# RMS norm with repeated rows: GpSimd in place of SyncE as the issuer of the loads of x and the stores

## The chip, the cores and the metric

The kernel runs on one core of a Trainium2 chip. The metric is device time in microseconds (us) of one execution. Before the change it was 238.1 us, the median of 3 runs (238.0 to 238.66). The engines are named as in the profile: DVE is VectorE, ACT is ScalarE, POOL is GpSimd, SP is SyncE; TensorE does no work in this kernel. An issue row of an engine's sequencer carries a q (SPq, POOLq).

## What is computed

```python
x: (8, 512, 2048) float32, gamma: (2048,) float32

def reference(x, gamma):
    x_rep = np.repeat(x, 2, axis=1)
    rms = np.sqrt((x_rep ** 2).mean(axis=-1, keepdims=True) + 1e-6)
    return ((x_rep / rms) * gamma[None, None, :]).astype(np.float32)
```

Each of 4,096 rows of 2,048 values is divided by its root mean square, multiplied by gamma, and written twice, to neighbouring rows of the output. 33.5 MB are read and 67.1 MB written.

## The kernel before

The rows lie in four blocks of 1,024 rows, numbered n = 0 to 3. A block is one load: each of the 128 partitions gets 8 neighbouring rows, 64 KB, in one transfer of 8.4 MB (`load`, L49 and L50). The output of a block is two stores, each of the doubled form of 4 rows per partition, again 64 KB per partition and 8.4 MB (`store`, L52 and L53). There are 4 loads and 8 stores, 12 transfers of one size.

All of it lives in one tile y of 24 rows of 2,048 values per partition, in three parts of 8 rows, `first` (rows 0 to 7), `second` (8 to 15) and `third` (16 to 23). `load(n, first + K)` fills rows 4 to 11, which is half of `first` and half of `second`; `load(m, third)` fills the third part. `squares` (L63, L67) sums the squares of a row on ACT and takes the root; `scale` (L76, L77) takes the reciprocal on DVE and multiplies the row by it and by gamma, writing the result to every second row of the target part; `repeat` (L84) copies these rows to the rows between, on ACT or on DVE.

The order is written by hand (`manual_schedule`), so that each engine takes its instructions as the code lists them. `four(n, m, constants, at_once)` handles two blocks: load n, the constants, load m, then rows 0 to 3 of n and store (n, 0), rows 4 to 7 and store (n, 1), and so for m. It is called with (0, 1) and then with (3, 2); the second call has no constants. In this text store (n, first half) is `store(n, 0, ...)`. The loads of the second call go to parts of y from which stores of the first call still read, and wait for those.

`constants()` brings gamma to one partition with four small DMAs on ACT's queue (one of 16 pieces of 500 bytes, L123, and three of 64 bytes, L129), into rows of y that are free at that time. POOL then spreads gamma to all partitions with two `partition_broadcast` instructions into gamma_b: L133 for the first 2,000 columns, which waits for the large piece, and L137 for the last 48, which waits for the small ones. In the code these stand between `load(n, ...)` and `load(m, ...)` of the first call. They are POOL's only work apart from four tiny fills and two configuration entries at the start.

Of the kernel before, what the change touches and what calls it, by code (L numbers as in the profile page):

```python
# [1 line left out]

# [4 lines left out]


@with_exitstack
def kernel(  # L10
    ctx: ExitStack,
    tc: tile.TileContext,
    x: bass.AP,
    gamma: bass.AP,
    out: bass.AP,
):
    nc = tc.nc
    P = nc.NUM_PARTITIONS
    f32 = mybir.dt.float32
    Act = mybir.ActivationFunctionType  # L20
    Alu = mybir.AluOpType

    B, S, D = x.shape
    Bo, So, Do = out.shape
    R = So // S
    assert R == 2 and D == Do and B == Bo and So == S * R
    eps = 1e-6
    inv_d = 1.0 / float(D)


    K = 4
    N = B * S
    ntiles = N // (P * K)
    assert N % (P * K) == 0 and ntiles == 8
    H = 2
    x_t = x.rearrange("b s d -> (b s) d").rearrange("(n p k) d -> n p k d", p=P, k=H * K)
    out_t = out.rearrange("b s d -> (b s) d").rearrange("(n p h j) d -> n h p (j d)", p=P, h=H, j=K * R)

    singles = ctx.enter_context(tc.tile_pool(name="singles", bufs=1))
    rows = ctx.enter_context(tc.tile_pool(name="rows", bufs=1))  # L40
    junk = ctx.enter_context(tc.tile_pool(name="junk", bufs=1, space=bass.MemoryType.PSUM))
    small = ctx.enter_context(tc.tile_pool(name="small", bufs=4))

    y = rows.tile([P, 3 * K * R, D], f32, name="y")
    first, second, third = 0, K * R, 2 * K * R

    def load(n, at):  # L49
        nc.sync.dma_start(out=y[:, at : at + H * K, :], in_=x_t[n])  # L50

    def store(n, h, to):  # L52
        nc.sync.dma_start(  # L53
            out=out_t[n, h], in_=y[:, to : to + K * R, :].rearrange("p j d -> p (j d)")
        )

    def squares(at, rows):

        n = len(rows)
        ss = small.tile([P, n], f32, name=f"ss{n}")  # L60
        for c, k in enumerate(rows):
            sq = junk.tile([P, D], f32, name="sq")
            nc.scalar.activation(  # L63
                out=sq[:], in_=y[:, at + k, :], func=Act.Square, accum_out=ss[:, c : c + 1]
            )
        rms = small.tile([P, n], f32, name=f"rms{n}")
        nc.scalar.activation(out=rms[:], in_=ss[:], func=Act.Sqrt, scale=inv_d, bias=eps_t[:])  # L67
        return rms

    def scale(at, to, rows, rms, at_once=K):  # L70
        n = len(rows)
        rstd = small.tile([P, n], f32, name=f"rstd{n}")
        for c, k in enumerate(rows):
            if c % at_once == 0:
                part = slice(c, min(c + at_once, n))
                nc.vector.reciprocal(out=rstd[:, part], in_=rms[:, part])  # L76
            nc.vector.scalar_tensor_tensor(  # L77
                out=y[:, to + R * k, :], in0=y[:, at + k, :], scalar=rstd[:, c : c + 1],
                in1=gamma_b[:], op0=Alu.mult, op1=Alu.mult,
            )  # L80

    def repeat(to, k0, k1, copy):
        y_r = y[:, to + R * k0 : to + R * k1, :].rearrange("p (k r) d -> p k r d", r=R)
        copy(out=y_r[:, :, 1, :], in_=y_r[:, :, 0, :])  # L84

    ctx.enter_context(tc.manual_schedule())

    half = K // 2
    up, down = list(range(K)), list(range(K - 1, -1, -1))

    def four(n, m, constants, at_once):


        load(n, first + K)
        constants()
        load(m, third)
        for rows, n_at_once in ((up[:half], half), (up[half:], at_once)):
            scale(first + K, first, rows, squares(first + K, rows), n_at_once)
        repeat(first, 0, half, nc.scalar.copy)
        repeat(first, half, K, nc.vector.tensor_copy)  # L100
        store(n, 0, first)
        scale(second, second, down, squares(second, down))
        repeat(second, half, K, nc.scalar.copy)
        repeat(second, 0, half, nc.vector.tensor_copy)
        store(n, 1, second)
        roots = [squares(third + h * K, up) for h in range(H)]
        scale(third, first, up, roots[0])
        repeat(first, 0, half, nc.scalar.copy)
        repeat(first, half, K, nc.scalar.copy)
        store(m, 0, first)  # L110
        scale(third + K, third, up, roots[1])
        repeat(third, 0, K, nc.scalar.copy)
        store(m, 1, third)

    gamma_b = singles.tile([P, D], f32, name="gamma_b")
    G, E = 16, 3
    C = D // G - E
    gamma_s = y[0:1, 0:2, :].rearrange("p k (c d) -> p (k c) d", c=G // 2)
    gamma_t = y[0:1, 2, :]
    eps_t = singles.tile([P, 1], f32, name="eps_t")  # L120

    def constants():
        nc.scalar.dma_start(  # L123
            out=gamma_s[0:1, :, :C],
            in_=gamma[: G * C].rearrange("(p c d) -> p c d", p=1, c=G),
        )
        for c in range(E):
            at = G * C + c * G
            nc.scalar.dma_start(  # L129
                out=gamma_t[0:1, c * G : (c + 1) * G],  # L130
                in_=gamma[at : at + G].partition_broadcast(1),
            )
        nc.gpsimd.partition_broadcast(  # L133
            out_ap=gamma_b[:, : G * C].rearrange("p (c d) -> p c d", c=G),
            in_ap=gamma_s[0:1, :, :C],
        )
        nc.gpsimd.partition_broadcast(out_ap=gamma_b[:, G * C :], in_ap=gamma_t[0:1, : E * G])  # L137
        nc.vector.memset(eps_t, eps)  # L138

        root = singles.tile([P, 1], f32, name="root")[:]  # L140
        nc.scalar.activation(out=root, in_=eps_t[:], func=Act.Sqrt)  # L141

    four(0, 1, constants, 1)
    four(3, 2, lambda: None, half)


# [1 line left out]
_INS = ['x', 'gamma']  # L148
_OUTS = [((8, 1024, 2048), 'float32')]


# [23 lines left out]
```

## Time and profile before

| | us |
|---|---|
| median of 3 runs | 238.1 |
| span of the profiled execution, first to last instruction | 236.3 |
| DVE busy | 84.5 |
| ACT busy | 110.2 |
| POOL busy | 2.8 |
| q1 (SP's queue: x and out) | 1,728 packets, 100.66 MB, 98.7% of 16 engines' span |
| q10 (ACT's queue: gamma) | 38 packets, 0.01 MB, 0.0% |
| loads of x, median from issue to landing | 31.4 |
| stores, median from issue to landing | 24.9 |
| HBM read and written | 33.56 MB, 67.11 MB: 426 GB/s over the span |

The span leaves out what lies before the first instruction and after the last one. The DMA share is the mean over the core's 16 DMA engines. A landing is the moment at which the transfer's semaphore is full; a transfer that stands behind others of its queue waits its turn within that time. Beside the page, the trace holds a record of each DMA packet (queue, size, start and duration).

### The profile page before, as it was taken

To read this page: it belongs to the slowest core of one execution; us is meant where nothing else is said; L and a number is where in the kernel's file an instruction comes from. 1 tells how busy PE (TensorE), PEld (TensorE's weight loads), DVE (VectorE), ACT (ScalarE), POOL (GpSimd) and SP (SyncE) were. 2 spreads that over 40 slices of the span, in tenths; PEclk is the share of its full clock that TensorE was granted. 3 is DMA by queue.
4 is the path that set the end of the run, shared out by engine and by line. 5 is a ranking of instruction groups with operands and counts; after the bars stand their busy time and mean duration, and the time that the engine had idled before them with its cause. 6 is when DMAs were issued, how large, how long until landed. Compare 5 with 4: busy or idle time off the path is not lost.

```text
span 236.3 us, 226 instructions
## 1 busy us (share of the span) xinstructions
DVE 84.5 (36%) x48; ACT 110.2 (47%) x86; POOL 2.8 (1%) x6
## 2 busy tenths in 40 slices
DVE  0000496594699500000000007928919992000000
ACT  2001989479998470000000049991999957400000
POOL 0110000000000000000000000000000000000000
DMA  9898989989898989989898998989898988989894
GB/s 355 356 533 355 521 366 477 411 366 521 355 533 356 499 388 466 422 366 521 355 533 355 488 399 355 533 355 533 355 533 355 499 388 377 510 355 533 355 533 178
DMA packets 1767, 100.68 MB, mean 426 GB/s; under 512 B 230, under 2 KB 230, under 8 KB 230
## 3 DMA queue, kind: packets, MB, share of 16 engines
q1 hardware_dynamic: 1728, 100.66, 98.7%
q10 hardware_dynamic: 38, 0.01, 0.0%
q14 instruction: 1, 0.01, 0.0%
HBM read 33.56 MB, written 67.11 MB: 426 GB/s over the span
## 4 chain that ended last, share of the span: by engine, by line
DMA 45%; ACT 26%; DVE 12%; issue 2%; DVEq 0%
DMA y<-in_x_dram 26%; DMA out_dram<-y 20%; ACT sq L63 15%; DVE y L77 12%; ACT y L84 11%; ACT rms L67 1%; DVE rstd L76 0%; DVEq L77 0%
## 5 line engine op out<-in xcount | busy, mean ns | idle before, releaser
L63 ACT ACTIVATE sq<-y 128x2048 f32<-128x2048 f32 x32 | 60.1, 1878 | 71.1 <-DMA y<-in_x_dram 70.4
L77 DVE SCALAR_TENSOR_TENSOR y<-y,rstd,gamma_b 128x2048 f32<-128x2048 f32 x32 | 73.8, 2349 | 1.6 <-DMA out_dram<-y 1.0
L84 ACT COPY y<-y 128x4096 f32<-128x4096 f32 (+1 forms) x10 | 42.6, 4284 | 19.1 <-DVE y L77 18.3
L76 DVE RECIPROCAL rstd<-rms 128x4 f32<-128x4 f32 (+2 forms) x11 | 1.9, 169 | 109.2 <-ACT rms L67 109.2
L84 DVE COPY y<-y 128x4096 f32<-128x4096 f32 x4 | 9.2, 2294 | 0.1
L63 ACT ACTIVATION_READ_ACCUMULATOR sq<-y 128x1 f32 x32 | 6.0, 186 | 0.0
L67 ACT ACTIVATE rms<-ss,eps_t 128x4 f32<-128x4 f32 (+1 forms) x10 | 3.0, 297 | 0.3
L141 ACT ACT_TABLE_LOAD x1 | 1.3, 1283 | 2.6 <-issue 2.6
L133 POOL PARTITION_BROADCAST gamma_b<-y x1 | 2.2, 2243 | 10.2 <-DMA y<-in_gamma_dram 10.2
L137 POOL PARTITION_BROADCAST gamma_b<-y x1 | 0.3, 323 | 10.1 <-DMA y<-in_gamma_dram 10.1
L138 DVE MEMSET eps_t<- 128x1 f32 x1 | 0.1, 59 | 0.8 <-PEq L159 0.8
L141 ACT ACTIVATE root<-eps_t 128x1 f32<-128x1 f32 x1 | 0.2, 203 | 0.0
L159 POOL MEMSET const-uint8-127<- 128x1 uint8 x1 | 0.1, 102 | 0.0
L159 POOL MEMSET const-bfloat16-1.0<- 128x1 bf16 x1 | 0.1, 101 | 0.0
L159 POOL MEMSET const-float32-0.0<- 128x1 f32 x1 | 0.1, 98 | 0.2 <-issue 0.2
L159 POOL MEMSET const-float32-1.0<- 128x1 f32 x1 | 0.1, 98 | 0.0
## 6 DMA issues: line engine op xcount, KB each, us to landing
out_dram<-y SPq DMA_DIRECT2D x8, 24.9
y<-in_x_dram SPq DMA_DIRECT2D x4, 31.4
y<-in_gamma_dram ACTq DMA_DIRECT2D x3, 0.1 KB
y<-in_gamma_dram ACTq DMA_DIRECT2D x1, 7.8 KB, 9.9
```

What stands on the lines that cost most here:

```text
L63: nc.scalar.activation(out=sq[:], in_=y[:, at + k, :], func=Act.Square, accum_out=ss[:, c : c + 1])
L67: nc.scalar.activation(out=rms[:], in_=ss[:], func=Act.Sqrt, scale=inv_d, bias=eps_t[:])
L76: nc.vector.reciprocal(out=rstd[:, part], in_=rms[:, part])
L77: nc.vector.scalar_tensor_tensor(out=y[:, to + R * k, :], in0=y[:, at + k, :], scalar=rstd[:, c : c + 1], in1=gamma_b[:], op0=Alu.mult, op ...
L84: copy(out=y_r[:, :, 1, :], in_=y_r[:, :, 0, :])
L133: nc.gpsimd.partition_broadcast(out_ap=gamma_b[:, : G * C].rearrange("p (c d) -> p c d", c=G), in_ap=gamma_s[0:1, :, :C],)
L137: nc.gpsimd.partition_broadcast(out_ap=gamma_b[:, G * C :], in_ap=gamma_t[0:1, : E * G])
L138: nc.vector.memset(eps_t, eps)
L141: nc.scalar.activation(out=root, in_=eps_t[:], func=Act.Sqrt)
L159: nc = _bacc.Bacc("TRN2", target_bir_lowering=False, num_devices=1)
```

## The change

`load` and `store` call `nc.gpsimd.dma_start` where they called `nc.sync.dma_start`. Shapes, sizes, the order in the code and everything else stay. The four DMAs of gamma stay on ACT's queue.

```diff
     def load(n, at):
-        nc.sync.dma_start(out=y[:, at : at + H * K, :], in_=x_t[n])
+        nc.gpsimd.dma_start(out=y[:, at : at + H * K, :], in_=x_t[n])
 
     def store(n, h, to):
-        nc.sync.dma_start(
+        nc.gpsimd.dma_start(
             out=out_t[n, h], in_=y[:, to : to + K * R, :].rearrange("p j d -> p (j d)")
         )
```

## The prediction

> **What bounds the kernel now.** I read first the busy slices of the page, the queues and the chain of waits.
>
> ```profile
> span 236.3 us, 226 instructions
> ...
> DVE 84.5 (36%) x48; ACT 110.2 (47%) x86; POOL 2.8 (1%) x6
> ...
> DMA  9898989989898989989898998989898988989894
> ...
> q1 hardware_dynamic: 1728, 100.66, 98.7%
> ...
> DMA 45%; ACT 26%; DVE 12%; issue 2%; DVEq 0%
> ```
>
> The DMA row is full from the first slice to the last, while no compute engine is busy for even half the span. The chain names ACT for 26%, but it is one path through work that runs under transfers; the row that decides is q1, whose packets take 98.7% of all 16 engines' time.
>
> The trace's DMA records make this exact. x and out move as 1536 packets of 65,536 bytes, 128 to a transfer, so each engine serves 8 packets of each of the 12 transfers. A packet takes 2.418 us, and 8 x 2.418 = 19.3 us is one transfer. The first packet starts at 1.73 us and the last ends at 235.08. Between these, one transfer's packets start where the last one's end: the first and the last of the 16 engines leave load(0) at 21.66 and 22.32, load(1) at 40.99 and 41.68, and so on to 234.60 and 235.08. 96 x 2.418 = 232.1 us of the 233.4 us between first start and last end is data. So only two things can change the time: a later (or earlier) first packet, and a hole in this row of packets. Compute matters solely where it releases a transfer too late.
>
> The second view is the timeline, for when each transfer is issued, and what POOL does meanwhile.
>
> ```profile
> 0.72 0.85 SPq L50 DMA_DIRECT2D y<-in_x_dram  x2
> 0.73 0.60 ACTq L123 DMA_DIRECT2D y<-in_gamma_dram  x1
> 1.36 1.21 ACTq L129 DMA_DIRECT2D y<-in_gamma_dram  x3
> 10.67 2.24 POOL L133 PARTITION_BROADCAST gamma_b<-y  x1 [10.24 <-DMA y<-in_gamma_dram]
> 22.97 0.32 POOL L137 PARTITION_BROADCAST gamma_b<-y  x1 [10.06 <-DMA y<-in_gamma_dram]
> 39.27 48.17 SPq L53 DMA_DIRECT2D out_dram<-y  x4
> 100.11 19.85 SPq L50 DMA_DIRECT2D y<-in_x_dram  x2
> 155.33 48.29 SPq L53 DMA_DIRECT2D out_dram<-y  x4
> ```
>
> Each line gives start, length, engine and instruction. SP issues both first loads at once, POOL waits for gamma until 22.97, and the later transfers go out at 39.27 to 87.1, 100.1 and 119.6, 155.33 to 203.3. SP waits for data, never for an engine that is behind with issuing.
>
> **The change, part by part.** Twelve issues leave SP and go to POOL. SP loses 12 instructions of 0.33 to 0.43 us each (rows L50 and L53), which were worth nothing: SP has no other work. Three places can feel it.
>
> (1) *The first load.* Between the start of SP's issue (0.72) and the first packet (1.73) lie 1.01 us. POOL's first instruction after the opening barrier stands at 0.80, so 0.08 later. What POOL needs from issue to first packet, call it L, no row shows. Below it is bounded by SP's 1.01, if issuing is equally quick. Above, take SP's 1.01 plus a whole POOL program of the longer kind seen, L133's 2.24: L = 3.25. The shorter kind, L137's 0.32, would make it 1.33. A transfer is 128 packets plus 16 completions, few things to write, but for 16 engines at both ends; I place it between the two, a little nearer the short one, at about 1.0 extra: L = 2.0. Cost: 0.08 + 1.0 = 1.1 us, wholly on the path, since nothing else occupies the engines then. The same bounds give 0.1 to 2.3.
>
> [...]
>
> (2) *The other eleven issues.* POOL pays L where SP paid 1.01, but with a backlog in front. What matters is the engine that finishes last, as it sets the end. Store (0, first half) is issued at 39.27 and the last engine comes free at 41.68: room for an L of 2.41. Store (3, first half) is issued at 155.33, the last engine comes free at 157.81: room for 2.48. These two are the tightest; the others have more (store (1, first half) at 76.17 against 80.32, load(3) at 100.1 against 119.1, load(2) at 119.6 against 138.5). A later start moves load, compute and store together, so the room stays. At L = 2.0 the cost is nothing, and the cover is the tail of load(1) and load(2); at L = 3.25 that cover is gone and it costs 0.84 + 0.77 = 1.6.
>
> (3) *load(1) is moved past POOL's two broadcasts.* In the code load(1) stands behind constants(), so on POOL it is queued behind L133 and L137, which wait for gamma. At the old times it could not be issued before 22.97 + 0.32 = 23.29, while the engines leave load(0) at 21.66 to 22.32. That is a hole unless gamma comes sooner. I think it does. Gamma was late because its small packets took turns with x: in the records its 500-byte packets start at 7.14, after two x packets, and engine by engine one gamma record and one x packet alternate, to 22.06. Now x starts at 0.80 + 2.0 = 2.8, while the four gamma issues still begin at 0.73 to 2.30 and, with the same 1.01, start moving at 1.7 to 3.3. The large piece and most of the three small ones would be through before x begins. If only the last piece (two records) falls behind, it is done after some three x packets, 2.8 + 3.1 (the first packets' mean) + 2 x 2.4 = 10.7; if all three small pieces (six records) fall behind, at 2.8 + 3.1 + 6 x 2.42 = 20.4, then 20.4 + 0.32 + 2.0 = 22.7, still ahead of the last engine's 22.32 + 1.1 = 23.4. So I cost (3) at nothing; its upper bound is the rival below. VectorE's use of gamma_b (27.3) lies behind load(0) either way.
>
> What stands queued behind a POOL wait is only the next transfer in the order SP had. The end (SP's wait for the last landing, 0.8 us of closing barrier) is unchanged. Sum: 1.1 + 0 + 0 = 1.1 us, a span of 236.3 + 1.1 = 237.4. The span lies 1.8 us under the median of the runs, 238.1, and that part is not touched: 239.2. With L from 1.6 to 2.6 the forecast's own range is 238.8 to 240.1 (at 2.6: 1.67 + 0.19 + 0.12 = 2.0).
>
> **Rivals.**
>
> *POOL issues about as fast as SP* (L under 1.6): the change does what it says and it cannot be told from none. For it: 128 packets are little to describe. Against: x then starts early and gamma lands late again. 238.1 to 238.8; say 238.5.
>
> *The hole at load(1).* Gamma stays behind x as now. At L = 1.0, load(1) moves at 23.29 + 0.08 + 1.0 = 24.4 against a last engine free at 22.4: 2.0, in sum 2.1, 240.2. At L = 2.0 all of it shifts by 1.1: 24.4 + 2.0 = 26.4 against 23.4, in sum 4.1, 242.2. Midway, 241.2. Against it: the four gamma issues do not move, while x starts later, and SP's second load issue no longer overlaps them.
>
> *Slow issue*, L = 2.6 to 3.25: 240.1 to 242.0 (2.3 + 1.6 = 3.9); at 2.9, 241.0.
>
> [...]
>
> [...]
>
> *VectorE shuts POOL out.* If POOL cannot write its work down while VectorE runs, store (1, first half), issued at 76.17, waits until L77's run ends at 80.03, and starts at 82.0 against 80.32; its twin waits to 196.21 and starts at 198.2 against 196.44: 1.7 + 1.8, and 239.2 + 3.5 = 242.7. Against: there are breaks between those instructions, and one of 2.35 us is covered by the 4.15 us of room. The copies at L84 can't matter: the stores wait for them.
>
> [...]
>
> *Smaller pieces.* If POOL cuts a packet in two, 96 more records an engine of at least 9 ns (the completion records) are 0.9 us: 240.1; in sixteen, 96 x 15 x 9 ns = 13 us: 252.
>
> *Faster.* The first packets take 3.1 us in place of 2.42, and the change from stores to load(3) and load(3) itself lose another 0.33 and 0.10 us (19.65 and 19.41 in place of 19.32): with the first 0.6, some 1.0 us that isn't data. If those belong to the way SP's queue starts and POOL's has none, and L is 1.01, the time is 238.1 + 0.1 - 1.0 = 237.2; from L = 1.25 on, less than 0.7 us of it is left. Nothing in the profile ties them to the queue; reads and writes changing over explain them as well.
>
> **How the numbers follow.** About 0.3%, 0.7 us, is what a measurement of this kernel can tell from no change. Chances: forecast 0.50, equally fast 0.22, hole 0.08, slow issue 0.05, code 0.05, VectorE 0.03, pieces 0.03, faster 0.04. So faster 0.04, same 0.22, slower 0.74. The range of 238.1 to 241.8 takes in the forecast, nearly all of "equally fast", half of the hole and most of slow issue; left out are faster, code, VectorE, sixteen pieces and the rest of the hole.
>
> **What would show it.** The first x packet near 2.8 us, all of load(0) shifted by as much; gamma's L133 starting well before 10.67, L137 well before 22.97; load(1) issued before about 20; packets of 65,536 bytes at 2.418 us, and no hole near 41 and 157. The prediction is wrong if the first packet comes before 2.3 or after 3.4, if load(1)'s first packet comes after 24, or if the packets become smaller or slower.

## The result, and the profile after

The changed kernel takes 241.05 us, the median of 4 runs (240.79 to 241.74), against 238.11; the ratio is 1.0114, 95% interval 1.009 to 1.0138. That is 2.9 us slower where 1.1 was forecast. The profiled execution has a span of 239.5 us against 236.3.

From the page of the changed kernel: span, busy times, the DMA slices and the queue that now carries x and out.

```profile
span 239.5 us, 226 instructions
...
DVE 84.5 (35%) x48; ACT 110.2 (46%) x86; POOL 9.3 (4%) x18
...
DMA  7999898989898989999999998989898989899894
...
q0 software_dynamic: 1728, 100.66, 97.9%
```

DVE and ACT do the same work in the same time as before. The 1,728 packets of x and out stand on another queue, q0, with the same number of bytes, and the DMA engines still decide: 97.9% in place of 98.7%. POOL's 6.5 us more are its twelve issues, 0.53 to 0.67 us each, which count as busy here.

The timeline of POOL, the column order as before.

```profile
1.26 0.67 POOL L50 DMA_DIRECT2D y<-in_x_dram  x1 [0.83 <-PEq L170]
2.87 2.24 POOL L133 PARTITION_BROADCAST gamma_b<-y  x1 [0.94 <-DMA y<-in_gamma_dram]
13.61 0.32 POOL L137 PARTITION_BROADCAST gamma_b<-y  x1 [8.50 <-DMA y<-in_gamma_dram]
14.10 0.57 POOL L50 DMA_DIRECT2D y<-in_x_dram  x1 [0.16 <-issue]
40.53 0.54 POOL L53 DMA_DIRECT2D out_dram<-y  x1 [25.87 <-ACT sq L63]
...
102.14 0.53 POOL L50 DMA_DIRECT2D y<-in_x_dram  x1 [13.38 <-DMA out_dram<-y]
...
158.46 0.54 POOL L53 DMA_DIRECT2D out_dram<-y  x1 [36.28 <-ACT sq L63]
```

Gamma is spread at 2.87 and 13.61 in place of 10.67 and 22.97, and load(1) goes out at 14.10, long before the engines need it at 22.5. Store (0, first half) goes out at 40.53; before it was 39.27.

Where the time went can be read from the trace's DMA records. A record does not name its engine, so I gave each packet to the engine whose packet before it ended nearest to its start. Figures in this table are us per engine, means over the 16 unless said otherwise; "excess" is packet time over 2.418 us a packet.

| | before | changed | more |
|---|---|---|---|
| first packet starts (median engine) | 1.85 | 2.86 | 1.01 |
| excess in the first packet | 0.70 | 0.58 | -0.12 |
| holes ahead of store (0, first half) and store (3, first half) | 0 | 0.13 + 0.21 | 0.34 |
| excess in the next three stores, (0, first half) to (1, first half) | 0.01 | 0.30 | 0.29 |
| excess at the turn from stores to loads: store (1, second half) and load(3) | 0.27 | 0.95 | 0.69 |
| excess in load(2) and the last four stores | 0.01 | 0.36 | 0.35 |
| last packet ends (median engine) | 234.79 | 237.29 | 2.51 |
| from the last engine's last packet to the end of the span | 1.18 | 1.62 | 0.43 |

The rows in between add up to 2.6, the measured shift is 2.5; with the tail it is 2.9. (In this execution the slowest engine lost 0.25 more than the median one, which makes the span's 3.2.) So the start, which the prediction had as the whole loss, is a third of it. More than half, some 1.7 us, comes from the middle, where the engines were never short of work for long.

What the middle looks like shows in the DMA row of a short window, 36 to 48 us in slices of 0.3 us. In slices shorter than a packet, a packet is counted where it starts, so a 9 marks slices in which several engines begin one, and the groups should stand 2.42 us, eight slices, apart. First the kernel before, then the changed one.

```profile
DMA  9990000099900000599000005995000059950000
```

```profile
DMA  0009990000099900000099000000990000009900
```

Before, each group is three to four slices wide throughout. In the changed kernel the third group, the first packets of store (0, first half), is narrow: it begins nine slices after the last one began, and the early engines have waited until the first can start at 42.0. By the records the 16 engines leave load(1) within 0.59 us of each other and start the store within 0.43.

### The profile page after: what moved, and what is told of

It is laid out like the page before. It is cut to its first block, busy times and chain, and to the rows that moved or that the text cites. A ratio compares the mean times of both kernels' runs of the same rounds, so it can differ in the third digit from the quotient of the medians.

```text
span 239.5 us, 226 instructions
## 1 busy us (share of the span) xinstructions
DVE 84.5 (35%) x48; ACT 110.2 (46%) x86; POOL 9.3 (4%) x18
## 3 DMA queue, kind: packets, MB, share of 16 engines
q0 software_dynamic: 1728, 100.66, 97.9%
## 4 chain that ended last, share of the span: by engine, by line
DMA 36%; issue 23%; ACT 14%; DVE 13%; POOL 1%; POOLq 0%; DVEq 0%; PEldq 0%
DMA y<-in_x_dram 26%; DVE y L77 11%; DMA out_dram<-y 10%; ACT sq L63 10%; ACT y L84 3%; DVE y L84 2%; POOL out_dram L53 1%; ACT rms L67 1%; DVE rstd L76 0%; POOLq L170 0%; POOLq L53 0%; POOLq L50 0%; DVEq L77 0%; PEldq L170 0%
## 5 line engine op out<-in xcount | busy, mean ns | idle before, releaser
L77 DVE SCALAR_TENSOR_TENSOR y<-y,rstd,gamma_b 128x2048 f32<-128x2048 f32 x32 | 73.8, 2348 | 1.7 <-DMA out_dram<-y 1.1
L84 ACT COPY y<-y 128x4096 f32<-128x4096 f32 (+1 forms) x10 | 42.6, 4283 | 19.1 <-DVE y L77 18.4
L53 POOL DMA_DIRECT2D out_dram<-y x8 | 4.3, 534 | 154.3 <-ACT sq L63 62.1
L84 DVE COPY y<-y 128x4096 f32<-128x4096 f32 x4 | 9.2, 2294 | 0.1
L50 POOL DMA_DIRECT2D y<-in_x_dram x4 | 2.3, 577 | 33.3 <-DMA out_dram<-y 32.4
L133 POOL PARTITION_BROADCAST gamma_b<-y x1 | 2.2, 2244 | 0.9 <-DMA y<-in_gamma_dram 0.9
L137 POOL PARTITION_BROADCAST gamma_b<-y x1 | 0.3, 323 | 8.5 <-DMA y<-in_gamma_dram 8.5
```

The source lines that it names most:

```text
L50: nc.gpsimd.dma_start(out=y[:, at : at + H * K, :], in_=x_t[n])
L53: nc.gpsimd.dma_start(out=out_t[n, h], in_=y[:, to : to + K * R, :].rearrange("p j d -> p (j d)"))
L77: nc.vector.scalar_tensor_tensor(out=y[:, to + R * k, :], in0=y[:, at + k, :], scalar=rstd[:, c : c + 1], in1=gamma_b[:], op0=Alu.mult, op ...
L133: nc.gpsimd.partition_broadcast(out_ap=gamma_b[:, : G * C].rearrange("p (c d) -> p c d", c=G), in_ap=gamma_s[0:1, :, :C],)
```

## Experiments

The ratios are to the kernel before on the same chip. Where transfers are divided between POOL and SP, the diff gives the condition by which `load` and `store` choose their queue.

**Only load(0) on POOL.**

```diff
+        queue = nc.gpsimd if n in (0,) else nc.sync          # load
-        nc.sync.dma_start(out=y[...], in_=x_t[n])
+        queue.dma_start(out=y[...], in_=x_t[n])
```

> Only load(0) is issued by POOL, the other eleven transfers by SP. Theory (four separate losses: the start, ragged holes before the first store of each half, slower packets in transfers that POOL issues, and POOL's closing drain): only the start remains, first packet near 2.6 us against 1.73, packets of the other transfers back at 2.418 us, 1.2 us from the last packet to the end of the span; 0.9 us over before, ratio 1.004. Rival (the packets are slower, or the tail longer, as soon as POOL has issued anything at all, or because of the run): ratio 1.008 or more, with 2.43 us packets in stores that SP issued.

Measured: 257.35 us, ratio 1.0809 (1.0794 to 1.0824). Both expectations missed, since I had left out what the common queue gave: load(0) served whole before load(1), landed at 22.65. Timeline of this run:

```profile
1.21 0.86 POOL L51 DMA_DIRECT2D y<-in_x_dram  x1 [0.78 <-PEq L172]
...
39.79 0.32 POOL L139 PARTITION_BROADCAST gamma_b<-y  x1 [24.60 <-DMA y<-in_gamma_dram]
41.93 1.88 ACT L65 ACTIVATE sq<-y 128x2048 f32<-128x2048 f32 x1 [37.83 <-DMA y<-in_x_dram]
```

With load(0) on POOL's queue and load(1) on SP's, the engines served both by turns, and load(0) landed at 41.9, when both were through, in place of 22.65. ACT's first square (L65 here) began 19 us late, and the engines then stood idle for 18 us until the first store. A side finding helps below: the stores behind this long hole, all issued by SP, run 6 to 13 ns a packet over 2.418 us in the first half.

**All on POOL but load(0).**

```diff
+        queue = nc.gpsimd if n in (1, 2, 3) else nc.sync     # load
+        queue = nc.gpsimd                                    # store
```

> load(0) by SP, all others by POOL. Theory (gamma came early in the changed kernel only because x started later): gamma's small packets are behind x again, L137 runs near 23 us, load(1) is issued near 23.5, its first packet comes near 25, and the engines stand idle for 2.3 to 3 us after load(0); no start loss; in sum with the slower packets (1.2) and the tail (0.4) some 4 us over before, ratio 1.017. Rival (gamma's delay has nothing to do with the start of x, only with SP's second load issue): L137 before 15, no hole, ratio 1.007.

Measured: 243.44 us, ratio 1.0231 (1.0217 to 1.0245). Timeline of POOL in this run:

```profile
10.62 2.24 POOL L135 PARTITION_BROADCAST gamma_b<-y  x1 [10.19 <-DMA y<-in_gamma_dram]
22.99 0.32 POOL L139 PARTITION_BROADCAST gamma_b<-y  x1 [10.13 <-DMA y<-in_gamma_dram]
23.52 0.68 POOL L51 DMA_DIRECT2D y<-in_x_dram  x1 [0.21 <-issue]
```

Gamma is as late as before the change, load(1) waits behind the broadcasts and starts at 24.91; the engines lose 3.1 us on average. So the rival "hole at load(1)" is real, and the changed kernel escapes it only because x starts later there. The size, 5.3 us, is more than the 4 expected, and two parts of it were new: the first packets of load(1) took 0.64 us longer, and its last ones 3.65 us in place of 2.42. And one thing spoke against the theory of slow packets on POOL's queue: the three stores behind, issued by POOL, ran at 2.418 us. The last four, behind holes of 0.01 us on average, lost 0.16 us in all.

**The last store on SP**, all else on POOL.

```diff
+        queue = nc.gpsimd                                            # load
+        queue = nc.sync if (n, h) == (2, 1) else nc.gpsimd           # store
```

> All as in the changed kernel, but the very last store is issued by SP. Theory (POOL's closing drain waits for POOL's last transfer and adds 0.4 us behind it): the drain ends early, 1.2 us from the last packet to the end, 0.4 us less than the changed kernel, about 240.6, ratio 1.0105 at most. Rival (the closing costs more once POOL has issued DMAs, whatever the last one is): 1.6 us, 241.0, ratio 1.012.

Measured: 240.79 us, ratio 1.0104 (1.0089 to 1.012); the medians alone don't separate it from the changed kernel's. The profiles do. The closing drains of POOL, first of the changed kernel, then of this run (shortest, median and longest in ns, first and last start):

```profile
L170 POOLq DRAIN  x3: 34/102/32638, 206.1 to 239.2; - x3
```

```profile
L172 POOLq DRAIN  x3: 34/96/33793, 195.9 to 239.4; - x3
```

The long drain starts beside POOL's last issue and lasts until that transfer is done: 206.1 + 32.6 = 238.7 in the changed kernel, 0.9 us behind the last packet, and 195.9 + 33.8 = 229.7 here, well before the end. (POOL's last transfer here is store (2, first half); it took turns with SP's store and landed at 229.2.) From last packet to end of span it is 1.21 us here, and 1.16 to 1.34 in every run whose last store SP issued; 1.47 to 1.69 where POOL did.

**The last four stores on POOL**, all else on SP.

```diff
+        queue = nc.sync                                              # load
+        queue = nc.gpsimd if n in (3, 2) else nc.sync                # store
```

> The four stores of the second half are issued by POOL, everything else by SP. Theory: no start loss; holes of up to 0.9 us on the engines that come free first before store (3, first half), next to none on the last one; packets of the last four transfers 2.425 to 2.435 us in place of 2.418, 0.3 us an engine; tail 0.4 more; 0.7 to 0.9 us over before, ratio 1.003 to 1.004. Rival (the slower packets come only where stores give way to loads, not from who issues): packets 2.418 in the last four, ratio 1.002.

Measured: 239.83 us, ratio 1.0073 (1.0061 to 1.0086). The packets of these stores are at 2.418 us, as the rival had it, but the first ones, at the change of queue, take 1.29 us longer, which neither had. So the slow packets follow neither POOL nor the second half. What they had followed so far were holes.

**The changed kernel without a copy ahead of the stores.** The part left out is VectorE's copy of rows 2 and 3 ahead of store (0, first half) and store (3, first half).

```diff
         repeat(first, 0, half, nc.scalar.copy)
-        repeat(first, half, K, nc.vector.tensor_copy)
         store(n, 0, first)
```

> The changed kernel without VectorE's copy ahead of store (0, first half) and store (3, first half): rows 2 and 3 of the four are not repeated there, and the two stores are released 2.3 us earlier. Theory (POOL's longer way from release to first packet opens holes at these two stores, and the holes make the packets behind them slower): no holes, stores at 2.418 us a packet, the turn from stores to load(3) as before the change (some 25 ns a packet over 2.418); left are the start, 0.9, and the tail, 0.4: 239.4, ratio 1.0055. Rival (packets that POOL issues are slower by themselves): holes gone but packets still 2.425 to 2.435 us, ratio 1.010 to 1.011.

Measured: 240.89 us, ratio 1.0102 (1.008 to 1.0124). The holes are gone, and with them the slow packets: 0.01 us of excess over the first three stores in place of 0.30, 0.05 at the turn to load(3) in place of 0.95, 0.01 in the last four stores. By the middle the theory is right and POOL's packets aren't slower. But the time is the rival's, since the last packets of load(1) take 1.08 us longer, the thing first seen with all on POOL but load(0).

**The kernel before with later stores**, all on SP.

```diff
         repeat(first, half, K, nc.vector.tensor_copy)
+        repeat(first, half, half + 1, nc.vector.tensor_copy)
         store(n, 0, first)
```

> The kernel before, all transfers on SP, with one more VectorE copy of one row (about 1.2 us) ahead of store (0, first half) and store (3, first half), which are released that much later. Theory (holes make the packets behind them slower, whoever issues): SP's stores at 2.425 to 2.435 us a packet, a dearer turn to load(3) (90 ns a packet in the transfer before it, against 24), no loss at the start or the end; 1.0 to 1.6 us over before, ratio 1.004 to 1.007. Rival (the slow packets belong to POOL's issuing): packets at 2.418, the last engine hardly touched, ratio 1.000 to 1.001.

Measured: 239.84 us, ratio 1.0059 (1.0038 to 1.0081), 1.6 us. Its DMA row in the window from 36 to 48:

```profile
DMA  5990000059900000099900000099000000990000
```

The groups close up behind the late store as in the changed kernel. Excess is 0.24 us in the three stores, 0.89 at the turn to load(3), 0.25 in the last four; holes 0.22 and 0.53. These packets were all issued by SP: what POOL's issuing does in the middle is to come 1 us late.

**load(0) and load(1) on POOL**, the rest on SP.

```diff
+        queue = nc.gpsimd if n in (0, 1) else nc.sync                # load
+        queue = nc.sync                                              # store
```

> load(0) and load(1) by POOL, the other ten transfers by SP: the start alone, with no second queue in flight beside load(0). Theory: first packet near 2.65 against 1.73, gamma early, load(1) without a hole, SP's stores on time: 0.9 over before, ratio 1.004; if the change of queue at store (0, first half) costs as it did in the run with the last four stores on POOL (1.3 us on the first packet), 2.2 over, ratio 1.009. Rival (the start is absorbed by slack later on): ratio 1.000.

Measured: 239.84 us, ratio 1.0059 (1.0036 to 1.0083). The first packet starts at 2.62, and load(1) leaves the last engine at 42.60 against 41.68: 0.92 us, not absorbed. The first packets of store (0, first half), the first on SP's queue, take 0.81 us longer, and the tail is 1.34. The rival is out; the size lies between the two numbers given.

**The changed kernel once more**, with no edit.

> The changed kernel once more, on the chip of these three: ratio 1.011 to 1.013; holes at store (0, first half) and store (3, first half), and 2.425 to 2.435 us a packet behind them, as in its first profile. If these packets were an accident of one run, they are at 2.418 here.

Measured: 241.42 us, ratio 1.0126 (1.0101 to 1.0151). Holes of 0.18 and 0.38, excess 0.33, 1.07 and 0.34 at the same three places: no accident of one run.

**The kernel before without the copy**, all on SP; the same part is left out as above.

```diff
-        repeat(first, half, K, nc.vector.tensor_copy)
         store(n, 0, first)
```

> The kernel before, all on SP, without VectorE's copy ahead of store (0, first half) and store (3, first half): these stores are released 2.3 us earlier, at about 37.0 and 153.0. Theory (a store that is queued before the engines begin the last load packet stretches that packet, and the kernel before just misses this): the last packets of load(1) take about 1.1 us longer, the later turn to load(3) costs nothing; 0.7 to 0.9 us over before although less work is done and the store comes earlier, ratio 1.003 to 1.004. Rival (the stretch in the run without the copies on POOL belongs to POOL): packets at 2.418, ratio 1.000.

Measured: 239.66 us, ratio 1.007 (1.0057 to 1.0084). Less work, an earlier store, and 1.6 us slower. Timeline line of the stores, and the DMA row from 36 to 48:

```profile
37.03 0.35 SPq L53 DMA_DIRECT2D out_dram<-y  x1
```

```profile
DMA  9955000099770000000099550000995500009995
```

The group that begins at 38.4, the last packets of load(1), is followed by the next only at 42.0, twelve slices later: each of these packets takes 3.4 to 3.9 us. The turn to load(3) then costs 0.03 us in place of 0.27. So the stretch isn't POOL's either. In the profiled execution the mean engine lost 0.9, as forecast; the one that finished last, 1.5 us behind the median, had left load(1) last and lost another 0.32 us at the start of load(3) and 0.69 at the end of load(2).

**The changed kernel with half the copy**: one row in place of two; the other row is left out.

```diff
-        repeat(first, half, K, nc.vector.tensor_copy)
+        repeat(first, half, half + 1, nc.vector.tensor_copy)
```

> The changed kernel with VectorE's copy ahead of store (0, first half) and store (3, first half) cut to one row: the stores are released 1.1 us earlier, which is what POOL takes longer than SP from release to first packet. Theory: the engines see these stores when they saw them before the change, so no holes, no stretched last load packet, stores at 2.418 us; left are the start, 0.9, the tail, 0.4, and some 0.3 at the turn to load(3) as before: 239.5, ratio 1.0055. Rival (POOL's issuing costs something else as well): ratio 1.008 or more.

Measured: 240.49 us, ratio 1.0095 (1.0082 to 1.0109). The expected 1.0055 is not reached. In its profile (239.98 us, the lowest of its four times) there are no holes, and the stores have 0.02 us of excess, as expected; but the last packets of load(1) take 0.37 us longer on average, 0.73 on the worst engine, and the tail is 1.69. Shifting the release by POOL's delay doesn't quite restore the old place; the remaining 0.5 us between this profile and the median of the runs is open. By the number the rival came true (1.008 or more), so this run doesn't rule out that POOL's issuing costs something else as well.

**load(1) ahead of the broadcasts.**

```diff
         load(n, first + K)
-        constants()
         load(m, third)
+        constants()
```

> The changed kernel with load(1) issued on POOL ahead of the two broadcasts. Theory (the broadcasts cost nothing where they stand, since gamma is early): first packets of load(1) right behind load(0), as with the changed order, and the same time, ratio 1.011 to 1.013. Rival (load(1) behind the broadcasts costs part of the loss): ratio under 1.009.

Measured: 241.23 us, ratio 1.0128 (1.0113 to 1.0144): as the changed kernel. Behind the broadcasts load(1) lost nothing.

## Why the prediction came out as it did

The direction, the bound and the range held: 241.05 lies in 238.1 to 241.8. The forecast's own range, 238.8 to 240.1, did not hold it, and the sum was too small by 1.8 us. That the range held the time is in part luck: its upper end was there for a slow issue and for a hole at load(1), and neither came. Two of the prediction's own signs failed: packets of 2.418 us, and no hole near 41 and 157.

*Part (1), the start: right.* L for load(0) is 2.62 - 0.80 = 1.8, forecast 2.0, and 0.8 above SP's 1.01; the first packet is 0.89 later, the last engine leaves load(0) 0.77 later, forecast 1.1. The run with load(0) and load(1) on POOL shows that it is not absorbed.

*Part (3), load(1) behind the broadcasts: right,* in the result and in the reason. L133 ran at 2.87 and L137 at 13.61, moving load(1) ahead of them changed nothing, and with x starting at 1.74 the hole was there.

*Part (2), the other eleven issues: the step that failed.* It said: "What matters is the engine that finishes last", and at L = 2.0 "the cost is nothing". L was not the fault: from the end of VectorE's copy to the first packet it is 2.07 us at store (0, first half) and 1.69 at store (3, first half), inside the room of 2.41 and 2.48. Taken literally the premise held: at store (0, first half) the last engine left load(1) at 42.43 and the last first packet of the store began at 42.46, at store (3, first half) at 160.51 and 160.51. But the engines that come free first did wait (the first left load(2) at 158.95, and no packet of the store began before 159.58), and I counted that as harmless. It wasn't: 0.34 us of holes a mean engine, and 1.3 us of slower packets behind them. SP does the same when its store is late by 1.2 us, and POOL doesn't when its store is early; these two runs settle that the lateness is the cause, and not the queue. How a hole of a fraction of a us makes later packets slower isn't settled. That the engines then start closer together doesn't explain it: in the last four stores of the kernel before they stood within 0.48 us of each other, with packets of 2.418 us, and in store (0, first half) of the run with the last store on SP within 0.78, with packets of 2.434.

*The end: wrong.* "Unchanged" left out POOL's closing drain, which waits for POOL's own last transfer: 0.43 us.

Together: 0.9 for the start, some 1.7 for the late stores and what follows (the late stores on SP alone cost 1.6), 0.4 for the tail: 3.0, where the runs lost 2.9.

*The rivals.* "Equally fast" and "slow issue" fell with L = 1.8. "Code", the 0.05 for a delay ahead of POOL's first work, did not come either: POOL's first issue starts at 1.26 and takes 0.67 us, the two configuration entries follow at 2.0, and L133 starts at 2.87. "VectorE shuts POOL out" did not happen either: store (1, first half) went out at 77.17, in the middle of L77's run from 71.62 to 80.89, in 0.53 us like the others. Beside VectorE's copies (L84) no issue ran: the four end 0.57 to 0.58 us ahead of the stores that wait for them. "Smaller pieces": the packets kept their 65,536 bytes. "Faster": the first packets' excess stayed, 0.58 against 0.70 us.

## What to carry to other kernels

Where the DMA engines have no gap, ask at each issue that ends a wait how far ahead of the first free engine it comes, and not of the last: here two stores that came some 1 us late cost 0.34 us in holes ahead of them and 1.3 in slower packets behind. The window is narrow on both sides here: the runs in which SP issued store (0, first half) 1.25 us later (40.52 in place of 39.27) and 2.24 us earlier (37.03) lost 1.6 us each. So this kernel has been placed by its release times, and both edits that moved them, one to each side, cost time. Moving load(0) alone to another queue gave up its order with load(1): 257.35 us, by far the dearest edit tried.

## What the runs showed of the hardware that was not expected

- At the turn from load(1) to store (0, first half), a store that was issued before the engines began the last packets of the load stretched these packets by 1.1 to 1.2 us (three runs: 1.08, 1.22, 1.23). In the kernel before, SP issued it at 39.27, just after they began (38.56 to 39.22), and the stretch was 0.02. It is not so at every turn: in two of the three runs store (3, first half) was also issued early, at 154.43 and 155.68, the last packets of load(2) beginning from 155.63 and 156.41, and these took only 0.12 and 0.06 us longer. What the engines do in that time, the records don't tell.
- Where that stretch occurred, the later turn from stores to load(3) cost 0.02 to 0.05 us; where load(1) passed into store (0, first half) without it and without a change of queue, 0.26 and 0.27, and 0.88 to 1.10 behind holes. In these runs the cost of changing direction seems to be paid at one place or the other; why is open.
- Where the queue changed between a load and a store, the first packets on the new queue were 0.81 and 1.29 us longer (two runs), more than all engines paid at the start of the kernel, 0.55 to 0.71. Where it changed beside traffic of the same direction, load(0) beside load(1) and the last store beside the one ahead of it, they were 0.01 and 0.00 us longer. So the change of queue alone didn't cost it in these two places.
- load(0) on POOL's queue and load(1) on SP's were served by turns: load(0) landed at 41.9 in place of 22.65.
